# A shared tile for two constants and a gap of 192 bytes: a decoder trunk whose tiles move to other starts in each SBUF partition

## The chip, the core and the metric

The kernel runs on one core of a Trainium2 chip. The metric is the time of one execution on the device in microseconds (us). A NeuronCore has a matrix engine (TensorE: PE for the matmuls, PEld for the loads of their stationary operand), a vector engine (VectorE: DVE), a scalar engine (ScalarE: ACT), GpSimd (POOL), and SyncE (SP), which here issues the DMA transfers. They work side by side and wait for one another on semaphores. Operands lie in SBUF, a memory of 128 partitions; a tile takes the same stretch of bytes in each partition. Matmuls write to PSUM.

## The reference

Two layers of a decoder trunk on 256 tokens of width 2048, float32 throughout. Each sub-layer is `x <- x + gate * f(RMSNorm(x) * (1 + scale) + shift)`, and shift, scale and gate come from a conditioning vector through a large matrix.

```python
cond = jax.nn.silu(c)
for l in range(DEPTH):                                  # 2 layers
    mod = cond @ ada_w[l] + ada_b[l]                    # 2048 -> 6 * 2048
    sh1, sc1, g1, sh2, sc2, g2 = jnp.split(mod, 6, axis=-1)
    h = modulate(rmsnorm(x, norm_mix_g[l]), sh1, sc1)
    y = mixer_ab(h, ...) if l % 2 == 0 else mixer_c(h, ...)
    x = x + g1[:, None, :] * y
    h = modulate(rmsnorm(x, norm_ffn_g[l]), sh2, sc2)
    x = x + g2[:, None, :] * swiglu(h, ffn_w1[l], ffn_w3[l], ffn_w2[l])
return rmsnorm(x, final_g)

def swiglu(h, w1, w3, w2):                              # 2048 -> 5632 -> 2048
    return (jax.nn.silu(h @ w1) * (h @ w3)) @ w2
```

`mixer_ab` is a product with a 2048 x 4096 matrix, a causal convolution over 31 tokens on one half, a gated mixing of tokens on the other, and a product with a 2048 x 2048 matrix. `mixer_c` is a pooling over 2, 4, 8 and 16 tokens and four products with 512 x 512 matrices. Nearly all the work is products of 256 tokens with weight matrices that are read once from the chip's main memory (HBM).

## The kernel before

**Products in three terms.** `load` brings 256 rows x 512 columns of a weight matrix (512 KB) into a tile `raw` of 4096 bytes in each partition; twelve such buffers are in use. `split` cuts it into two float32r tiles: ACT rounds `raw` to `hi` (L206), DVE takes `lo = raw - hi` (L207); four buffers each. The activations are cut in the same way: `ah` and `al` for the inputs of a sub-layer, `mh` and `ml` in the same places for the inner activations of the mixers, `hh` and `hl` for the hidden activations of SwiGLU. For each block of 128 x 128 activations, TensorE loads the block as the stationary operand (LDWEIGHTS, 512 bytes in each partition) and streams 512 columns of weights past it (MATMUL, the moving operand, 2048 bytes in each partition). The three products are high by high (L255), high weights by low activations (L256), and low weights by high activations (L261). So one half of `unit` (one `raw`) is 12 matmuls: for each of two token blocks twice L255 and L256, then four of L261. Rows of the profile name `out<-moving,stationary`: `mm<-hi,hh` streams `hi` past `hh`. `mm` and, in places, `mt` are the PSUM results.

**Stages.** An opening in a written order (conditioning vector, first norms); `mixer_ab` (up to some 440 us); SwiGLU of layer 0 (to about 1190 us); `mixer_c`; SwiGLU of layer 1. In SwiGLU the products with `w1` and `w3` have `ah` and `al` as stationary operands, those with `w2` have `hh` and `hl`. Beside the main products run steps of the conditioning products: on PE (L354, L420) or on DVE (L392, L427), handed out by a credit that `tick` counts.

**Where tiles lie.** Pools are laid out one after the other in each partition in the order in which `__init__` opens them: constants, `x` (residual), `act` (`ah`, `al`, and `mh`, `ml` in the same places), `raw`, `whi` (`hi`), `wlo` (`lo`), `acc`, `gate`, `work`; then a pool of the stage, which for SwiGLU holds `hh` and `hl`, 2048 bytes each. A tile takes its bytes rounded up to 32, so a constant of 4 bytes takes 32. In the program as built, the starts modulo 512 bytes are:

| tiles | before | after |
|---|---|---|
| `ident`, `identr`, `ones` (128 columns each) | 160 | 160 |
| `x`, `ah`/`al`/`mh`/`ml`, `raw`, `hi`, `lo`, `acc`, `gate` | 32 | 0 |
| work tiles `xr`, `gy`, `hm`, `s1` (2048 bytes) | 32 | 192 |
| work tiles `rows`; `h32` | 352; 96 | 0; 256 |
| `hh`, `hl` (SwiGLU), and the bands for `mixer_c` in the same places | 352 | 0 |
| in `mixer_ab`: `aT`, the convolution's input; `co`, its output | 352; 288 | 0; 448 |

The blocks of an activation tile lie 512 bytes apart and the two halves of a weight tile 2048, so all of one family's operands share the start of their family. `mhalf` (-0.5) is read by POOL for the power in `rstd` (L518); `pick` (ones in rows 0, 32, 64, 96) is the moving operand of one column in `put_cols` (L448).

Of the kernel before, what the change touches and what calls it, by code (L numbers as in the profile page):

```python
# [8 lines left out]
F32 = mybir.dt.float32  # L9
# [8 lines left out]
P = 128  # L18
# [22 lines left out]
class Trunk:  # L41
# [6 lines left out]
    def __init__(self, ctx, tc, ins, out):  # L48
        self.ctx, self.tc, self.nc = ctx, tc, tc.nc
        self.i, self.out = ins, out  # L50
        self.bg = []
        self.credit = 0.0
        self.late = []
        self.fill = []
        self.lean = False

        def pool(name, bufs, **kw):
            return ctx.enter_context(tc.tile_pool(name=name, bufs=bufs, **kw))

        self.cpool = pool("const", 1)  # L60
        self.xpool = pool("resid", 1)
        self.apool = pool("act", 1)
        self.rawp = pool("raw", RAW)
        self.hip = pool("whi", HL)
        self.lop = pool("wlo", HL)
        self.accp = pool("acc", 1)
        self.gp = pool("gate", 2)
        self.wk = pool("work", 2)
        self.mmp = pool("mmp", 4, space=PSUM)
        self.tpp = pool("tpp", 2, space=PSUM)  # L70
        self.adap = pool("adap", 1, space=PSUM)
        self.msp = pool("msp", 1, space=PSUM)


    def consts(self):
        nc, c = self.nc, self.cpool
        i = self.i
        warm = c.tile([P, 1], F32, name="warm")
        nc.vector.memset(warm, 0.0)
        nc.scalar.activation(warm, warm, AF.Silu)  # L80
        self.ident = c.tile([P, P], F32, name="ident")
        make_identity(nc, self.ident)
        self.identr = c.tile([P, P], F32R, name="identr")
        nc.vector.tensor_copy(self.identr, self.ident)
        self.ones = c.tile([P, P], F32, name="ones")
        nc.vector.memset(self.ones, 1.0)
        self.mhalf = c.tile([P, 1], F32, name="mhalf")
        nc.gpsimd.memset(self.mhalf, -0.5)
        self.pick = c.tile([P, 1], F32, name="pick")
        nc.gpsimd.memset(self.pick, 0.0)  # L90
        for j in range(4):
            nc.gpsimd.memset(self.pick[32 * j : 32 * j + 1, :], 1.0)
# [1105 lines left out]
```

## Time and profile before

| what | value |
|---|---|
| runs | 2008.52, 2008.23, 2002.36 us; median 2008.23 us |
| the profiled execution | 2001.65 us, span of its instructions 1999.9 us |
| mean granted TensorE clock | 0.984 |
| matmuls | 8896, of which 7584 are of the three kinds L255, L256, L261 |
| moved by DMA | 540.39 MB, 537.79 MB of it on SP's queue |

The page of the profile gives, in this order: the busy time of each engine; the span in 40 equal slices, each digit the busy share in tenths; the DMA queues; the chain of work that ended last, followed back from the end, as shares of the span; the costliest groups of instructions by line and operands with their mean duration. A matmul's duration in these rows is from its start to the modelled end of its results; the next one starts before that, so the pace of a stream is read from the distance between starts in the timeline, not from the duration.

### The profile page before, as it was taken

The numbers are of one execution on the slowest core, as the hardware profiler recorded it, in microseconds if no ns is written. First come the engines' busy times: TensorE is split into PE (matmuls) and PEld (weight loads), VectorE is DVE, ScalarE is ACT, GpSimd is POOL, SyncE is SP. The second block draws the span as 40 slices with busy tenths as digits, with TensorE's granted clock in tenths as the row PEclk, the third lists the DMA queues.
The fourth block names the chain that finished last, engine by engine and source line by source line (L and its number), as shares of the span: only waits on it lengthen the run. The fifth ranks groups of instructions, "written<-read, shape, count | busy, mean of one in ns | idle before, by whom it ended". The sixth has DMA issues, their size and how long they took to land.

```text
span 1999.9 us, 24247 instructions
## 1 busy us (share of the span) xinstructions
PE 1950.2 (98%) x8896; PEld 1539.9 (77%) x8896; DVE 1408.9 (70%) x1650; ACT 849.8 (42%) x1047; POOL 33.9 (2%) x92
## 2 busy tenths in 40 slices
PE   6899999989999999999999999999999999999998
PEld 3566667768887888887878877888788888888886
DVE  2678999796878878777887788877455445554455
ACT  3244343465444334433344346544434444334443
POOL 0000000000000000000210000000000000000000
PEclk7899999989999999999999999999999999999999
DMA  9998988798989899888988887988556665566551
GB/s 350 366 358 281 339 273 277 277 343 278 322 299 327 314 311 347 313 295 304 327 325 297 281 289 264 332 280 309 194 189 190 190 190 191 178 196 192 189 184 48
DMA packets 246248, 540.39 MB, mean 270 GB/s; under 512 B 16521, under 2 KB 17849, under 8 KB 245744
## 3 DMA queue, kind: packets, MB, share of 16 engines
q1 hardware_dynamic: 245840, 537.79, 77.9%
q8 instruction: 69, 1.13, 0.2%
q10 hardware_dynamic: 288, 1.05, 0.1%
q14 instruction: 51, 0.42, 0.1%
HBM read 536.68 MB, written 2.10 MB: 269 GB/s over the span
## 4 chain that ended last, share of the span: by engine, by line
PE 93%; DMA 3%; DVE 2%; ACT 1%; issue 0%; SPq 0%; POOL 0%; POOLq 0%; DVEq 0%; ACTq 0%
PE mm L255 28%; PE mm L256 27%; PE mm L261 27%; PE ps_ada L420 1%; DMA raw<-in_ab_w_in_dram 1%; PE ps_col L448 1%; PE mt L255 1%; PE tp L699 1%; PE mt L256 1%; PE mt L261 1%; PE ps_ada L354 1%; PE tp L532 1%; DMA x<-in_x_dram 1%; DVE accq L427 1%; DMA raw<-in_ada_w_dram 1%; PE tp L965 1%
## 5 line engine op out<-in xcount | busy, mean ns | idle before, releaser
L206 ACT CAST hi<-raw 128x1024 fp32r<-128x1024 f32 x632 | 663.8, 1052 | 1010.9 <-PE mm L256 902.8
L207 DVE TENSOR_TENSOR lo<-raw,hi 128x1024 fp32r<-128x1024 f32 x632 | 771.0, 1224 | 426.0 <-ACT hi L206 419.2
L255 PE MATMUL mm<-hi,ah 128*128 128x512 f32 x1568 | 618.7, 395 | 4.7 <-ACT hi L206 3.7
L256 PE MATMUL mm<-hi,al 128*128 128x512 f32 x1568 | 613.5, 391 | 0.0
L261 PE MATMUL mm<-lo,ah 128*128 128x512 f32 x1568 | 422.1, 390 | 0.0
L255 PEld LDWEIGHTS mm<-hi,ah 128*128 128x128 f32 x1568 | 295.6, 189 | 89.3 <-ACT hi L206 16.0
L261 PEld LDWEIGHTS mm<-lo,ah 128*128 128x128 f32 x1568 | 295.0, 188 | 61.6
L256 PEld LDWEIGHTS mm<-hi,al 128*128 128x128 f32 x1568 | 296.0, 189 | 60.2
L255 PE MATMUL mm<-hi,hh 128*128 128x512 f32 x704 | 278.9, 396 | 0.0
L256 PE MATMUL mm<-hi,hl 128*128 128x512 f32 x704 | 278.1, 395 | 0.0
L392 DVE SCALAR_TENSOR_TENSOR acc<-raw,cond,acc 128x1024 f32<-128x1024 f32 x210 | 269.1, 1281 | 7.0 <-DMA raw<-in_ada_w_dram 5.1
L261 PE MATMUL mm<-lo,hh 128*128 128x512 f32 x704 | 194.7, 395 | 0.0
L255 PEld LDWEIGHTS mm<-hi,hh 128*128 128x128 f32 x704 | 132.0, 187 | 33.9 <-ACT hi L206 1.7
L261 PEld LDWEIGHTS mm<-lo,hh 128*128 128x128 f32 x704 | 132.0, 187 | 32.2
L256 PEld LDWEIGHTS mm<-hi,hl 128*128 128x128 f32 x704 | 132.1, 188 | 31.8
L803 DVE SCALAR_TENSOR_TENSOR co<-aT,cw,co 128x256 f32<-128x256 f32 x240 | 100.1, 484 | 0.0
L420 PE MATMUL ps_ada<-raw,cond 128*32 128x512 f32 x352 | 60.9, 659 | 6.4 <-DMA raw<-in_ada_w_dram 5.7
L255 PE MATMUL mm<-hi,mh 128*128 128x512 f32 x160 | 65.1, 408 | 1.6 <-ACT mh L541 1.6
L256 PE MATMUL mm<-hi,ml 128*128 128x512 f32 x160 | 64.6, 406 | 0.3 <-DVE ml L542 0.3
L707 DVE TENSOR_TENSOR gy<-mm,gate 128x512 f32<-128x512 f32 x72 | 47.0, 686 | 23.9 <-PE mm L261 23.6
L427 DVE SCALAR_TENSOR_TENSOR accq<-raw,cond,accq 128x512 f32<-128x512 f32 x75 | 56.3, 751 | 9.7 <-DMA raw<-in_ada_w_dram 7.8
L255 PE MATMUL mt<-hi,ah 128*128 128x512 f32 x96 | 40.7, 424 | 7.2 <-ACT hi L206 7.2
(170 smaller groups left out, 993.7 us busy)
## 6 DMA issues: line engine op xcount, KB each, us to landing
raw<-in_ffn_w_dram SPq DMA_DIRECT2D x528, 512.0 KB, 4.8
raw<-in_ada_w_dram SPq DMA_DIRECT2D x384, 512.0 KB, 5.6
raw<-in_ab_w_in_dram SPq DMA_DIRECT2D x64, 512.0 KB, 7.9
raw<-in_ab_w_out_dram SPq DMA_DIRECT2D x32, 512.0 KB, 6.6
raw<-in_pool_w_dram SPq DMA_DIRECT2D x8, 512.0 KB
x<-in_x_dram SPq DMA_DIRECT2D x2, 1024.0 KB
gate<-in_final_g_dram SPq DMA_DIRECT2D x1, 1024.0 KB
out_dram<-x SPq DMA_DIRECT2D x2, 512.0 KB, 3.8
```

What stands on the lines that cost most here:

```text
L206: nc.scalar.copy(hi, raw)
L207: nc.vector.tensor_tensor(lo, raw, hi.bitcast(F32), op=ALU.subtract)
L255: nc.tensor.matmul(ps[b], act[b][0][:, kk, :], hi[:, k, :], start=first and kk == 0, stop=False)
L256: nc.tensor.matmul(ps[b], act[b][1][:, kk, :], hi[:, k, :], start=False, stop=False)
L261: self.nc.tensor.matmul(ps[b], act[b][0][:, kk, :], lo[:, k, :], start=False, stop=last and kk == 3)
L354: nc.tensor.matmul(ps[32 * j : 32 * j + 32, :], self.cond[:, k : k + 1].to_broadcast([P, 32]), raws[j // 2][:, j % 2, :], start=k == 0, st ...
L392: nc.vector.scalar_tensor_tensor(acc, raw, self.cond[:, k : k + 1], acc, op0=ALU.mult, op1=ALU.add)
L420: nc.tensor.matmul(acc[32 * j : 32 * j + 32, :], self.cond[:, k : k + 1].to_broadcast([P, 32]), raws[j // 2][:, j % 2, :], start=u == 0, s ...
L427: nc.vector.scalar_tensor_tensor(acc, raws[j // 2][:, j % 2, :], self.cond[:, k : k + 1], acc, op0=ALU.mult, op1=ALU.add)
L448: nc.tensor.matmul(ps[:, a : a + 1], src[:, P * a : P * a + P], one, start=u == 0, stop=u == len(parts) - 1,)
L707: nc.vector.tensor_tensor(t, ps, g[:, 512 * q : 512 * q + 512], op=ALU.mult)
L803: nc.vector.scalar_tensor_tensor(co[:, k, :], src, cw[:, k, j : j + 1], co[:, k, :], op0=ALU.mult, op1=ALU.add,)
```

## The change

Two constants of 4 bytes, `mhalf` and `pick`, become the two columns of one tile `two`, so that the constants take 32 bytes less and all that follows moves down by 32 bytes. At the head of the pool `work` a tile `gap` of 192 bytes is reserved, which nothing reads or writes; with it the pool behind `work` begins 160 bytes further up than before. No instruction is added or taken away, and on every engine the instructions stand in the same order with the same waits; only the name `two` stands where `mhalf` and `pick` stood. The starts that result are in the table above.

```diff
@@ -66,6 +66,7 @@
         self.accp = pool("acc", 1)
         self.gp = pool("gate", 2)
         self.wk = pool("work", 2)
+        self.wk.tile([P, 48], F32, name="gap", tag="gap", bufs=1)
         self.mmp = pool("mmp", 4, space=PSUM)
...
@@ -84,9 +85,9 @@
         nc.vector.memset(self.ones, 1.0)
-        self.mhalf = c.tile([P, 1], F32, name="mhalf")
+        two = c.tile([P, 2], F32, name="two")
+        self.mhalf, self.pick = two[:, :1], two[:, 1:]
         nc.gpsimd.memset(self.mhalf, -0.5)
-        self.pick = c.tile([P, 1], F32, name="pick")
         nc.gpsimd.memset(self.pick, 0.0)
```

## The prediction

> **What bounds the kernel now.** I read the page from the top: busy shares, the slices, the chain.
>
> ```profile
> span 1999.9 us, 24247 instructions
> PE 1950.2 (98%) x8896; PEld 1539.9 (77%) x8896; DVE 1408.9 (70%) x1650; ACT 849.8 (42%) x1047; POOL 33.9 (2%) x92
> PE   6899999989999999999999999999999999999998
> DMA  9998988798989899888988887988556665566551
> PE 93%; DMA 3%; DVE 2%; ACT 1%; issue 0%; SPq 0%; POOL 0%; POOLq 0%; DVEq 0%; ACTq 0%
> ```
>
> PE is busy in 98% of the span, and only the first slices have holes. The chain that ended last lies on PE for 93% and on DMA for 3% (0.03 x 1999.9 = 60 us). The other engines matter only through what they hold up. So I need the pace of the matmul stream, and who works in it:
>
> ```profile
> L255 PE MATMUL mm<-hi,ah 128*128 128x512 f32 x1568 | 618.7, 395 | 4.7 <-ACT hi L206 3.7 <-ACT ah L541 1.0
> L255 PE MATMUL mm<-hi,hh 128*128 128x512 f32 x704 | 278.9, 396 | 0.0
> L255 PE MATMUL mm<-hi,mh 128*128 128x512 f32 x160 | 65.1, 408 | 1.6 <-ACT mh L541 1.6
> L255 PE MATMUL mt<-hi,ah 128*128 128x512 f32 x96 | 40.7, 424 | 7.2 <-ACT hi L206 7.2
> ```
>
> Each of these rows stands for three equal groups (L255, L256, L261). With `ah`/`al` or `mh`/`ml` as stationary operand there are 3 x (1568 + 160 + 96) = 5472 matmuls, with `hh`/`hl` 3 x 704 = 2112. The durations overlap, so they don't tell the pace. The timeline does: the group of four L261 returns every 12 matmuls. First and last rows of undisturbed stretches, `hh` twice, then `ah`, then `mh`:
>
> ```profile
> 640.30 1.09 PE L261 MATMUL mm<-lo,hh 128*128 128x512 f32 x4
> ...
> 679.50 1.09 PE L261 MATMUL mm<-lo,hh 128*128 128x512 f32 x4
> ```
>
> ```profile
> 1457.26 1.09 PE L261 MATMUL mm<-lo,hh 128*128 128x512 f32 x4
> ...
> 1513.26 1.09 PE L261 MATMUL mm<-lo,hh 128*128 128x512 f32 x4
> ```
>
> ```profile
> 551.88 1.07 PE L261 MATMUL mm<-lo,ah 128*128 128x512 f32 x4
> ...
> 568.20 1.07 PE L261 MATMUL mm<-lo,ah 128*128 128x512 f32 x4
> ```
>
> ```profile
> 398.10 1.07 PE L261 MATMUL mm<-lo,mh 128*128 128x512 f32 x4
> ...
> 411.70 1.07 PE L261 MATMUL mm<-lo,mh 128*128 128x512 f32 x4
> ```
>
> The stretches hold 14, 20, 6 and 5 returns. With `hh`: 39.20 / 14 = 2.80 us and 56.00 / 20 = 2.80 us for 12 matmuls, 233.3 ns each. With `ah`: 16.32 / 6 = 2.72 us; with `mh`: 13.60 / 5 = 2.72 us, 226.7 ns each. The same moving tiles `hi` and `lo` run 6.67 ns slower past one family of stationary operands than past the others. Is that other work beside it?
>
> ```profile
> 551.00:569.00 18.00, 18.00 (x81) 14.81 (x79) 8.02 (x7) 7.88 (x9) 0.00 (x0) 1.00 0.67 214
> 640.00:680.00 40.00, 40.00 (x173) 32.22 (x173) 32.83 (x32) 15.03 (x15) 0.00 (x0) 1.00 0.93 341
> 1457.00:1514.00 57.00, 57.00 (x246) 45.69 (x245) 30.81 (x31) 21.49 (x21) 0.00 (x0) 1.00 0.58 186
> ```
>
> (Stretch and its length; then busy time and, in brackets, instructions of PE, PEld, DVE, ACT, POOL; then granted clock, DMA share, GB/s.) No: the clock is 1.00 in all three, and `hh` goes at 2.80 us both beside 341 GB/s and a DVE at 82% and beside 186 GB/s and a DVE at 54%, while `ah` at 2.72 lies between them in DMA. Nor is the load of the stationary operand itself longer (minimum, median and maximum in ns, from the rows of L255):
>
> ```profile
> L255 PEld LDWEIGHTS mm<-hi,ah x1568: 186/188/330, 44.3 to 1920.7; 128*128 128x128 f32 x196
> L255 PEld LDWEIGHTS mm<-hi,hh x704: 186/187/192, 621.2 to 1989.2; 128*128 128x128 f32 x176
> ```
>
> What the layout sets apart is the start: `hi`, `lo`, `ah` and `mh` all begin at 32 modulo 512 bytes, `hh` at 352. A load of stationary values runs under the stream of the matmul before it, so both read SBUF at once; an offset of 320 between them seems to cost 6.67 ns a matmul, an offset of 0 does not.
>
> The Trainium skill, in "TensorE: Matmul & The Clock Gate", section "Back-to-back issue gap", gives a gap of N/2.4 + 2.5 ns for an isolated matmul on the full clock, 216 ns for 512 columns, with no term for where the operands lie. By it the change would be worth nothing on TensorE. The trace does not agree with it: 226.7 and 233.3 ns.
>
> **The change, part by part.**
>
> *The starts of `hh` and `hl`* go from 352 to 0, those of `hi` and `lo` from 32 to 0: the offset between them becomes 0, as it is now between `hi` and `ah`. Bounds: 0 (the pace has another cause) and the full difference, 2112 x 6.67 ns = 14.1 us. I take 14.1, since two families at offset 0 (`ah`, `mh`, with different data) keep 226.7 to the last digit. All of it lies on the path: PE is busy without a hole in both `hh` stretches. What is late next there: ACT's `hi` waits for PE, so it follows; DMA would have to give 341 x 2.80 / 2.72 = 351 GB/s in the first stretch, below what it gives in the opening (387 below).
>
> *The starts of `hi`, `lo`, `ah`, `al`, `mh`, `ml`* go together from 32 to 0. Their offset to each other stays 0. No row shows a family that starts at 0; the rows around are 226.7 (at 32) and 233.3 (at 352). Below, the quickest stream of loads and matmuls is the plain float32 one of the convolution's norm:
>
> ```profile
> 347.10 2.32 PE L813 MATMUL ps_ln<-co,ones 128*128 128x256 f32 x10
> L813 PE MATMUL ps_ln<-co,ones 128*128 128x256 f32 x16 | 3.9, 379 | 0.0
> ```
>
> Ten take 2.32 us, the last of them 0.38: (2.32 - 0.38) / 9 = 215.5 ns each, for half as many columns of another type, but one full load beneath each as here. So the ends for these 5472 are 5472 x (215.5 - 226.7) = -61 us and 5472 x (233.3 - 226.7) = +36.5 us. I take 0, the nearest row, their own: if the offset between two streams decides, nothing changes.
>
> *DVE and ACT.* All their operands move. L803 reads the convolution's input at starts that step by 4 bytes from tap to tap, and L207, between tiles that all start at 32, is as even:
>
> ```profile
> L803 DVE SCALAR_TENSOR_TENSOR co<-aT,cw,co x240: 432/483/510, 167.0 to 347.9; 128x256 f32<-128x256 f32 x120
> L207 DVE TENSOR_TENSOR lo<-raw,hi x632: 1211/1225/1362, 44.2 to 1979.5; 128x1024 fp32r<-128x1024 f32 x158
> ```
>
> Thirty starts, and all lie between 432 and 510 ns, so DVE hardly sees the start; for ACT no row varies it. The chain has DVE and ACT for 3% (60 us); 1% of that either way is 0.6 us. I take 0.
>
> *DMA.* Every `raw` is now written from a multiple of 512. What this brings shows only where a transfer is waited for, and that is the opening:
>
> ```profile
> ACT hi L206 <- DMA raw<-in_ab_w_in_dram: 42.3, 10, 11.2
> 0.00:20.00 20.00, 9.50 (x33) 2.15 (x33) 2.63 (x10) 7.62 (x20) 3.44 (x17) 0.90 0.90 337
> 20.00:40.00 20.00, 17.02 (x85) 8.72 (x87) 3.55 (x13) 5.59 (x11) 0.55 (x1) 0.67 0.97 344
> 40.00:60.00 20.00, 17.92 (x72) 11.40 (x72) 15.67 (x22) 6.68 (x10) 0.00 (x0) 0.75 1.05 387
> 60.00:80.00 20.00, 15.82 (x69) 10.60 (x62) 11.37 (x19) 7.37 (x11) 1.10 (x1) 0.83 0.98 334
> ```
>
> The rate is 337 to 387 GB/s at one and the same start. If all four stretches (mean 350.5) went at the best, the 60 us of DMA on the chain would shrink by 60 x (1 - 350.5/387) = 5.7 us; that is the end for a gain. If all went at the worst, it would grow by 60 x (350.5/334 - 1) = 3 us, the end for a loss. I take a gain of 1 us, near the middle.
>
> The Trainium skill ("DMA: Bandwidth & Descriptors", section "How a descriptor splits into AXI transactions") says that a piece that starts off a 256-byte boundary is cut at the boundary below: 2048 bytes from 32 would take 65 beats of 32 bytes instead of 64. By that, an estimate, the gain would be 60 / 65 = 0.9 us. No run here shows a transfer into SBUF from such a boundary.
>
> *The shared tile and the gap* add no instruction or wait. POOL's power and PE's one-column products read the same values; both constants are written once in the opening, in the same order on POOL. 0.
>
> *Transposes* read work tiles that start at 192 instead of 32, against `ident` at 160. The two large groups:
>
> ```profile
> L699 PE MATMUL tp<-ident,hm 128*128 128x128 f32 x176 | 23.1, 272 | 0.0
> L532 PE MATMUL tp<-ident,xr 128*128 128x128 f32 x96 | 18.5, 342 | 9.9 <-ACT xr L527 6.6 <-ACT xT L570 3.1
> ```
>
> At 6.67 ns each, either way, 272 of them are 2 us. I take 0.
>
> **The sum** is made against the profiled execution: 2001.65 - 14.1 - 1 = 1986.6 us. Runs shown reach from 2002.36 to 2008.52 with the median 6.6 us above the profiled time. Half of that on top gives 1990.
>
> **The rivals.**
>
> *The start itself decides, and 0 is good for all.* Then `ah` and `mh` gain too. For it: 226.7 is 11.2 ns above the 215.5 of L813, and everything in that stream starts off a 64-byte multiple (32, 352). Against it: 32 and 352 are equally odd for any line of 64 bytes, and yet differ. Halfway between the ends, 221 ns for all: 5472 x 5.6 + 2112 x 12.3 = 57 us, so 1945 us; at the end 61 + 2112 x 17.8 ns = 99 us, and DVE, at 82% in one stretch above, would take part of that back.
>
> *Nothing happens.* The `hh` tiles also lie in the last part of the partition, behind `work`, and stay there; if that, or their values, set the pace, only DMA's 1 us is left: 2001, or up to 2008 on the scale of the median.
>
> *Slower: 0 is the bad start.* If two streams that begin on the same 512-byte multiple hinder each other as 352 and 32 do now, `ah` and `mh` go to 233.3: 5472 x 6.67 = 36.5 us, and `hh` stays: 2038 us. It decides from the point where the 456 groups of 12 with `ah` or `mh` lose more than the `hh` groups and DMA bring: 15.1 us / 456 = 33 ns a group, 2.753 instead of 2.72. For it: no row shows a start at 0. Against it: `hi` and `ah` now also begin on the same place of their 512 bytes, and are the quicker ones.
>
> **How the numbers follow.** Offset decides, 1990: 0.60, between 1983 (DMA's full gain, on the profiled time) and 1997 (on the median, without DMA's). All gain, 1945: 0.16. Nothing: 0.15. Slower: 0.09. A measurement of this kernel can tell about 0.3%, 6 us. The range 1940 to 2008 leaves out the slower case and the far half of the all-gain case, 0.17 together. Faster by over 0.3%: 0.16, all but a little of 0.60, and 0.02 of "nothing" by scatter, 0.73; within: 0.18; slower: 0.09.
>
> **What would show it.** In the profile of the changed kernel: groups of L261 with `hh` every 2.72 us, those with `ah` and `mh` still at 2.72; the same 8896 matmuls; durations of L206 and L207 as now; the waits for `raw` in the opening within a few us of 42. The prediction is wrong if `hh` stays at 2.80 (the place in the partition or the data), or if `ah` leaves 2.72 in either direction (the start itself).

## The result, and the profile after

The changed kernel took 1985.13 us (median of four runs, 1983.53 to 1990.03) against 2006.13 for the kernel before (with a fourth run of 2004.03): a ratio of 0.9901, 95% interval 0.9875 to 0.9927. A second comparison of the same two kernels gave 0.9895 (0.9881 to 0.9910). The forecast was 1990 us, and 15.1 of 2001.65 us, 0.75%, by its sum; the ratio says 1.0%.

The page of the changed kernel, its span, PE's busy share, the chain and the group with `hh`:

```profile
span 1988.3 us, 24247 instructions
PE 1940.1 (98%) x8896; PEld 1541.6 (78%) x8896; DVE 1407.9 (71%) x1650; ACT 852.1 (43%) x1047; POOL 34.5 (2%) x92
PE 93%; DMA 3%; DVE 1%; ACT 1%; issue 0%; SPq 0%; POOL 0%; POOLq 0%; ACTq 0%; DVEq 0%
L256 PE MATMUL mm<-hi,hh 128*128 128x512 f32 x704 | 275.2, 391 | 0.0
```

The same instructions, the same bound. (One line was added to the code, so L255, L256, L261 and L206 of before are L256, L257, L262 and L207 here.) What changed is the pace past `hh`. The group of four `lo` matmuls returns every 12 matmuls. The first and the last such group of undisturbed stretches, with `hh`, then `ah`, then `mh`:

```profile
1452.22 1.07 PE L262 MATMUL mm<-lo,hh 128*128 128x512 f32 x4
...
1506.62 1.07 PE L262 MATMUL mm<-lo,hh 128*128 128x512 f32 x4
```

```profile
548.17 1.07 PE L262 MATMUL mm<-lo,ah 128*128 128x512 f32 x4
...
569.93 1.07 PE L262 MATMUL mm<-lo,ah 128*128 128x512 f32 x4
```

```profile
393.57 1.07 PE L262 MATMUL mm<-lo,mh 128*128 128x512 f32 x4
...
409.89 1.07 PE L262 MATMUL mm<-lo,mh 128*128 128x512 f32 x4
```

With `hh` 20 returns take 54.40 us, 2.72 each, where they took 2.80 before. `ah` (21.76 / 8) and `mh` (16.32 / 6) stay at 2.72. It is not the clock: the granted clock was 1.00 in the stretch with `hh`, as it was before (behind the five busy times, clock, DMA share and GB/s):

```profile
1452.00:1507.00 55.00, 55.00 (x244) 45.57 (x243) 30.82 (x31) 21.29 (x21) 0.00 (x0) 1.00 0.61 192
```

What that is worth in all can be read from the first write of an `hh` tile, which stands ahead of every matmul with `hh`, to the end of the span. First and last start of the 44 writes, before and then after:

```profile
L700 ACT CAST hh<-tp x44: 585/592/606, 513.6 to 1929.0; 128x512 fp32r<-128x512 f32 x44
L701 ACT CAST hh<-tp x44: 586/592/605, 515.2 to 1919.3; 128x512 fp32r<-128x512 f32 x44
```

1999.9 - 513.6 = 1486.3 us became 1988.3 - 515.2 = 1473.1: 13.2 us less, with a granted clock of 1.00 from there on in both. If each of the 2112 matmuls with `hh` or `hl` gave up the 6.67 ns it would be 14.1.

Ahead of that lies the opening. Stretches of 20 us there, last column GB/s:

```profile
0.00:20.00 20.00, 10.64 (x33) 2.81 (x33) 2.84 (x11) 7.88 (x21) 3.44 (x17) 0.91 0.90 348
20.00:40.00 20.00, 17.26 (x91) 7.99 (x91) 4.34 (x14) 7.33 (x15) 0.55 (x1) 0.70 0.95 360
40.00:60.00 20.00, 17.42 (x74) 11.52 (x72) 16.83 (x24) 4.68 (x6) 0.00 (x0) 0.79 1.05 406
60.00:80.00 20.00, 14.23 (x58) 9.36 (x59) 11.25 (x18) 7.57 (x11) 1.63 (x1) 0.83 0.94 330
```

337, 344, 387 and 334 became 348, 360, 406 and 330. Where the DMA engines are busy throughout (share over 1), 387 became 406, 5% more. The chain of waits through the opening, start and length of pieces that wait for weights, before and then after:

```profile
78.30 10.74 DMA raw<-in_ada_w_dram
89.10 10.76 DMA raw<-in_ab_w_in_dram
```

```profile
76.11 10.22 DMA raw<-in_ada_w_dram
86.39 10.22 DMA raw<-in_ab_w_in_dram
```

Each is 5% shorter, and the second ends at 96.6 us instead of 99.9. This lead of 3 us did not last. The same eight `hi` matmuls and the `lo` group behind them, before and then after, with the granted clock around them (the number ahead of the DMA share):

```profile
119.16 0.39 PE L255 MATMUL mm<-hi,ah 128*128 128x512 f32 x1
121.01 1.07 PE L261 MATMUL mm<-lo,ah 128*128 128x512 f32 x4
115.00:120.00 5.00, 3.23 (x13) 2.14 (x13) 4.86 (x8) 0.64 (x2) 0.00 (x0) 1.00 1.01 368
```

```profile
116.78 0.63 PE L256 MATMUL mm<-hi,ah 128*128 128x512 f32 x1
120.18 1.09 PE L262 MATMUL mm<-lo,ah 128*128 128x512 f32 x4
115.00:120.00 5.00, 4.04 (x10) 3.03 (x11) 4.89 (x8) 2.48 (x3) 0.00 (x0) 0.67 1.05 406
```

They begin 2.4 us earlier, but at a granted clock of 0.67 instead of 1.00 they take 3.40 us instead of 1.85, and 0.8 us of the lead is left. A later stretch took that too:

```profile
320.00:425.00 105.00, 103.14 (x487) 77.94 (x485) 90.50 (x121) 44.15 (x61) 1.61 (x1) 0.97 0.84 296
```

```profile
320.00:425.00 105.00, 103.14 (x475) 77.34 (x473) 90.40 (x121) 43.60 (x61) 1.61 (x1) 0.95 0.83 290
```

(Before, then after: 487 matmuls at a granted clock of 0.97, 475 at 0.95.) At the first `hh` this execution was 1.6 us behind the one before (515.2 and 513.6). The two profiled executions are therefore only 2001.65 - 1990.03 = 11.6 us apart, while the medians are 21.0. The one shown here is the longest of its four runs.

### The profile page after: what moved, and what is told of

Read it like the earlier page. It is cut to its first block, busy times and chain, and to the rows that moved or that the text cites. A ratio compares the mean times of both kernels' runs of the same rounds, so it can differ in the third digit from the quotient of the medians.

```text
span 1988.3 us, 24247 instructions
## 1 busy us (share of the span) xinstructions
PE 1940.1 (98%) x8896; PEld 1541.6 (78%) x8896; DVE 1407.9 (71%) x1650; ACT 852.1 (43%) x1047; POOL 34.5 (2%) x92
## 4 chain that ended last, share of the span: by engine, by line
PE 93%; DMA 3%; DVE 1%; ACT 1%; issue 0%; SPq 0%; POOL 0%; POOLq 0%; ACTq 0%; DVEq 0%
PE mm L256 28%; PE mm L257 27%; PE mm L262 27%; PE ps_ada L421 2%; PE ps_col L449 1%; DMA raw<-in_ada_w_dram 1%; PE tp L700 1%; PE mt L256 1%; PE mt L257 1%; PE mt L262 1%; PE ps_ada L355 1%; DMA raw<-in_ab_w_in_dram 1%; PE tp L533 1%; DMA x<-in_x_dram 1%; PE tp L966 1%
## 5 line engine op out<-in xcount | busy, mean ns | idle before, releaser
L207 ACT CAST hi<-raw 128x1024 fp32r<-128x1024 f32 x632 | 665.8, 1054 | 997.0 <-PE mm L257 892.8
L256 PE MATMUL mm<-hi,ah 128*128 128x512 f32 x1568 | 619.4, 395 | 4.7 <-ACT hi L207 3.7
L257 PE MATMUL mm<-hi,al 128*128 128x512 f32 x1568 | 614.1, 392 | 0.0
L262 PE MATMUL mm<-lo,ah 128*128 128x512 f32 x1568 | 422.2, 390 | 0.0
L256 PEld LDWEIGHTS mm<-hi,ah 128*128 128x128 f32 x1568 | 296.1, 189 | 90.3 <-ACT hi L207 15.1
L257 PEld LDWEIGHTS mm<-hi,al 128*128 128x128 f32 x1568 | 296.4, 189 | 60.3
L262 PEld LDWEIGHTS mm<-lo,ah 128*128 128x128 f32 x1568 | 294.9, 188 | 61.7
L256 PE MATMUL mm<-hi,hh 128*128 128x512 f32 x704 | 275.2, 391 | 0.0
L257 PE MATMUL mm<-hi,hl 128*128 128x512 f32 x704 | 274.2, 389 | 0.0
L262 PE MATMUL mm<-lo,hh 128*128 128x512 f32 x704 | 190.3, 389 | 0.0
L256 PEld LDWEIGHTS mm<-hi,hh 128*128 128x128 f32 x704 | 132.2, 188 | 29.6 <-ACT hi L207 1.7
L262 PEld LDWEIGHTS mm<-lo,hh 128*128 128x128 f32 x704 | 132.1, 188 | 27.6
L257 PEld LDWEIGHTS mm<-hi,hl 128*128 128x128 f32 x704 | 132.2, 188 | 27.1
L256 PE MATMUL mm<-hi,mh 128*128 128x512 f32 x160 | 65.1, 408 | 1.6 <-ACT mh L542 1.6
L257 PE MATMUL mm<-hi,ml 128*128 128x512 f32 x160 | 64.1, 403 | 0.3 <-DVE ml L543 0.3
L262 PE MATMUL mm<-lo,mh 128*128 128x512 f32 x160 | 47.3, 405 | 0.0
```

The source lines that it names most:

```text
L207: nc.scalar.copy(hi, raw)
L256: nc.tensor.matmul(ps[b], act[b][0][:, kk, :], hi[:, k, :], start=first and kk == 0, stop=False)
L257: nc.tensor.matmul(ps[b], act[b][1][:, kk, :], hi[:, k, :], start=False, stop=False)
L262: self.nc.tensor.matmul(ps[b], act[b][0][:, kk, :], lo[:, k, :], start=False, stop=last and kk == 3)
```

## The experiments

**The two edits apart.** Theory: the offset between the moving and the stationary operand decides. Rival: the multiple of 512 itself. The gap alone brings offset 0 without a multiple of 512 (`hi` and `hh` both at 32); the shared tile alone brings `hi` to 0 and leaves the offset at 320.

```diff
 # gap_only: before, with
+        self.wk.tile([P, 48], F32, name="gap", tag="gap", bufs=1)
 # two_only: before, with
+        two = c.tile([P, 2], F32, name="two")
+        self.mhalf, self.pick = two[:, :1], two[:, 1:]
```

> The gap of 192 bytes alone, the two constants in tiles of their own as before. `hi`, `lo`, `ah`, `raw` stay at 32 modulo 512, `hh` and `hl` go from 352 to 32. If the offset between the stationary operand and the moving one decides, groups of 12 matmuls with `hh` return every 2.72 us, and the kernel gains the 14.1 us of TensorE alone: ratio to the kernel before about 0.993. If the multiple of 512 itself decides, `hh` keeps 2.80 and the ratio is 1.000.

> The shared tile alone, no gap. `hi`, `lo`, `ah`, `raw` go to 0, `hh` and `hl` to 320: the offset between them stays 320. If the offset decides, `hh` keeps 2.80 us for 12 matmuls, `ah` 2.72, and what is left is the effect of writing `raw` to a multiple of 512: 1 us by the prediction (ratio 0.9995), up to 5.7 us (0.997) if the whole rest of the measured gain is that. If the start itself decides, `hh` changes its pace.

The gap alone: ratio 0.9936 (0.9922 to 0.9950). The shared tile alone: 0.9969 (0.9958 to 0.9979). `hh` in the timeline of each, 22 groups, first the gap alone, then the shared tile alone:

```profile
1450.83 1.07 PE L262 MATMUL mm<-lo,hh 128*128 128x512 f32 x4
...
1507.95 1.07 PE L262 MATMUL mm<-lo,hh 128*128 128x512 f32 x4
```

```profile
1450.18 1.09 PE L261 MATMUL mm<-lo,hh 128*128 128x512 f32 x4
...
1508.98 1.09 PE L261 MATMUL mm<-lo,hh 128*128 128x512 f32 x4
```

57.12 / 21 = 2.72 with the gap, 58.80 / 21 = 2.80 with the shared tile. The offset decides, and a start at 32 is as good as one at 0. From the first `hh` to the end the gap alone takes 1473.3 us, like the changed kernel, and the shared tile alone 1486.2, like the kernel before. So what the shared tile brings, by the ratio 2004 x 0.0031 = 6.2 us, lies ahead of the first `hh`: it comes at 509.2 us instead of 513.6 in the profiled executions. The two parts add up: 0.64% and 0.31% against the 1.0% of both.

**Which offsets are good.** Pads between the chunks of `hh` and `hl` give four offsets to `hi` in one kernel.

```diff
 # ffn, ahead of the tiles of chunk ci in the first group of layer 0
+                if gi == 0 and l == 0 and (BASE if ci == 0 else 64):
+                    p.tile([P, (BASE if ci == 0 else 64) // 4], F32, name=f"pad{ci}", tag=f"pad{ci}")
```

> The changed kernel with pads between the SwiGLU tiles, so that the four chunks of hidden activations start at 0, 64, 128 and 192 modulo 512, while `hi` and `lo` stay at 0. If two streams hinder each other in narrow places of the 512 bytes, only some of the four chunks run at more than 2.72 us for 12 matmuls. If any offset costs, three of the four do. If the part of the partition decides, all four run alike.

> As the kernel with starts 0 to 192, but the chunks start at 256, 320, 384 and 448 modulo 512. The offset theory expects 2.80 us for 12 matmuls at 320, as in the kernel before; for the others it has no number. If a start that is odd to 64 bytes was the cause (352 before), all four run at 2.72.

> The four chunks of hidden activations at 32, 96, 160 and 224 modulo 512, with `hi` and `lo` at 0. The scan in steps of 64 gave 226.7, 233.3, 232.3 and 229.9 ns a matmul at 0, 64, 128 and 192. If the cost rises and falls evenly, 32 lies between 226.7 and 233.3 and 224 between 229.9 and 226.7; if offset 0 is a single good place, all four lie at 230 to 233. One below 226.7 would be a better place than the changed kernel's.

Each chunk is two halves of 12 matmuls, so two returns of `lo` belong to one chunk; the distance inside a pair is that chunk's pace. Offsets 0, 64, 128, 192, a pair each:

```profile
1452.37 1.07 PE L262 MATMUL mm<-lo,hh 128*128 128x512 f32 x4
1455.09 1.07 PE L262 MATMUL mm<-lo,hh 128*128 128x512 f32 x4
1457.86 1.10 PE L262 MATMUL mm<-lo,hh 128*128 128x512 f32 x4
1460.66 1.09 PE L262 MATMUL mm<-lo,hh 128*128 128x512 f32 x4
1463.44 1.10 PE L262 MATMUL mm<-lo,hh 128*128 128x512 f32 x4
1466.24 1.08 PE L262 MATMUL mm<-lo,hh 128*128 128x512 f32 x4
1469.00 1.08 PE L262 MATMUL mm<-lo,hh 128*128 128x512 f32 x4
1471.75 1.08 PE L262 MATMUL mm<-lo,hh 128*128 128x512 f32 x4
```

2.72, 2.80, 2.80 and 2.75 us. In the second kernel the pair at 256:

```profile
1453.74 1.07 PE L262 MATMUL mm<-lo,hh 128*128 128x512 f32 x4
1456.46 1.07 PE L262 MATMUL mm<-lo,hh 128*128 128x512 f32 x4
```

2.72 again; its other three pairs repeat the first kernel's (2.81, 2.80, 2.75). So the pattern has a period of 256 bytes, and 320 before was 64. At 32, 96, 160 and 224, 17 groups from the third kernel:

```profile
1448.18 1.09 PE L262 MATMUL mm<-lo,hh 128*128 128x512 f32 x4
...
1493.00 1.10 PE L262 MATMUL mm<-lo,hh 128*128 128x512 f32 x4
```

44.82 / 16 = 2.80. Of the eight offsets modulo 256 that were tried, 0 alone runs at 2.72, and none is below. (A chunk lasts 24 matmuls and follows one at another offset; what a longer stretch at one offset, 192 above all, would hold was not run.) The kernels took 1994.01, 1995.37 and 1998.13 us, one run each.

**The same cost put on the other operands.** If the offset decides, it must also slow `ah` and `mh` when these are the ones left behind. (`self.hip`, `self.lop` and `self.accp` are the pools of `hi`, `lo` and `acc`; what is reserved at the head of a pool moves all that lies behind it.)

```diff
 # hi_gap192: after, with
         self.hip = pool("whi", HL)
+        self.hip.tile([P, 48], F32, name="gap_hip", tag="gap_hip", bufs=1)
 # lo_gap192: after, with 48 such elements at the head of self.lop and 16 at the head of self.accp
```

> The changed kernel with 192 bytes more ahead of `hi`: `raw` and `ah` stay at 0, while `hi`, `lo`, `hh` and all that follows start at 192 modulo 512. From `hi` to `ah` the offset is then -192, which is 64 modulo 256, the place at which the scan ran slow; from `hi` to `hh` it is 0. If the offset modulo 256 decides, `ah` and `mh` now take 2.80 us for 12 matmuls and `hh` 2.72: 36.5 us more than the changed kernel, about 2022 us, a ratio of 1.008 to 1.010 to the kernel before. If only the far tiles behind the work pool are sensitive, `ah` keeps 2.72 and the time is that of the changed kernel.

> The changed kernel with `lo` alone moved, to 192 modulo 512; `hi`, `raw` and `ah` at 0, `hh` at 256, which is 0 modulo 256 from `hi`. From `lo` to all stationary operands the offset is then 64 modulo 256. If the moving tile's offset to the stationary block that is loaded beneath it decides, the four matmuls that stream `lo` run at 233.3 ns and the eight that stream `hi` at 226.7: 2.75 us for 12, 16.9 us more in all, about 2002 us. If the bare position of `hh` or `ah` decides, nothing changes.

With `hi` and `lo` moved, `ah` (9 groups) and `hh` (20 groups):

```profile
548.87 1.09 PE L263 MATMUL mm<-lo,ah 128*128 128x512 f32 x4
...
571.27 1.09 PE L263 MATMUL mm<-lo,ah 128*128 128x512 f32 x4
...
1454.76 1.08 PE L263 MATMUL mm<-lo,hh 128*128 128x512 f32 x4
...
1506.44 1.07 PE L263 MATMUL mm<-lo,hh 128*128 128x512 f32 x4
```

22.40 / 8 = 2.80 and 51.68 / 19 = 2.72: the roles are exchanged. The time is 2018.85 us (ratio 1.0071, 1.0050 to 1.0092), 34 us above the changed kernel's 1984.58; 5472 x 6.67 ns would be 36.5. With `lo` alone moved:

```profile
1649.81 0.40 PE L259 MATMUL mm<-hi,al 128*128 128x512 f32 x1
...
1651.42 1.09 PE L264 MATMUL mm<-lo,ah 128*128 128x512 f32 x4
1652.35 0.39 PE L258 MATMUL mm<-hi,ah 128*128 128x512 f32 x1
```

The four that stream `lo` take 0.93 us, 232.5 ns each, as expected. But the seven of `hi` ahead of them take 1.61, 230.0 ns each and not 226.7: after a stretch of bad offset it takes some matmuls until the good pace is back. So the 12 take more than the 2.75 us expected:

```profile
1453.25 1.09 PE L264 MATMUL mm<-lo,hh 128*128 128x512 f32 x4
...
1505.82 1.09 PE L264 MATMUL mm<-lo,hh 128*128 128x512 f32 x4
```

52.57 / 19 = 2.767 us. Over all 632 groups of 12 that would be 29.5 us; the one run took 2008.10 us, 18 to 25 us above the runs of the changed kernel, where 16.9 were expected. So the tile that streams matters and not only the one that is loaded; how the delay carries over stays open.

**What a transfer needs.** `raw` (pool `self.rawp`) at 64 and at 256 modulo 512, the operands of the main products at offset 0 modulo 256 to each other.

```diff
 # raw64: after, with 16 elements at the head of self.rawp and 48 at the head of self.hip
 # raw256: after, with 64 elements at the head of self.rawp
```

> The changed kernel with `raw` at 64 modulo 512, and `hi`, `lo`, `hh` at 256, so that their offset to `ah` stays 0 modulo 256. TensorE keeps 2.72 us for 12 matmuls with all. If it takes a multiple of 256 for a transfer to be quick, as the Trainium skill has it (page DMA: Bandwidth & Descriptors), the opening is as slow as with the start at 32 and the ratio to the kernel before is 0.993 to 0.994, as with the gap alone; if a multiple of 64 is enough, it is 0.990 to 0.991.

> As the kernel with `raw` at 64, but at 256 modulo 512. If a multiple of 256 is enough for DMA and an offset of 256 is 0 for TensorE, the ratio is that of the changed kernel, 0.990; if it takes 512, 0.993 to 0.994.

Ratios 0.9925 (0.9911 to 0.9938) and 0.9912 (0.9896 to 0.9928), whose intervals overlap. The opening tells them apart, GB/s in the last column; first 64, then 256:

```profile
40.00:60.00 20.00, 17.61 (x80) 10.66 (x74) 15.42 (x21) 6.43 (x10) 0.00 (x0) 0.81 1.05 387
80.00:100.00 20.00, 15.58 (x78) 10.08 (x76) 12.65 (x18) 2.09 (x2) 0.00 (x0) 0.91 1.05 387
```

```profile
40.00:60.00 20.00, 15.62 (x74) 9.48 (x72) 16.26 (x21) 4.61 (x5) 0.00 (x0) 0.97 1.05 406
80.00:100.00 20.00, 14.51 (x71) 8.96 (x70) 14.85 (x19) 4.67 (x5) 0.00 (x0) 0.89 1.05 408
```

387 is the rate of the start at 32, 406 to 408 that of the start at 0. The other runs agree: in these two stretches all three kernels with `raw` at 32 or 64 show 387, and all nine with it at 0 or 256 show 401 to 408. A multiple of 64 is not enough, one of 256 is; 128 was not tried. The Trainium skill ("DMA: Bandwidth & Descriptors", section "How a descriptor splits into AXI transactions") puts the boundary at 256 bytes too, but speaks of bytes that are fetched, and here it is the destination that moved. An estimate by its count of beats, 65 from 32 and 66 from 64 against 64, is 1.6% and 3%; the runs show 5% at both.

In the time it is harder to see. In the profiled executions the first `hh` is written at 513.6 (before), 513.9 (gap alone) and 517.8 us (`raw` at 64), and at 515.2 and 512.8 (changed kernel, twice), 514.7 (`raw` at 256) and 509.2 (shared tile alone): the two sets overlap, and the executions differ in the clock that was granted (0.982 to 0.986 on the mean).

**Is there more to have?** All the remaining large tiles at 0 as well, beside the changed kernel on the same chip.

```diff
 # all0: after, without the gap in work; gs.., sh.., cond, adab, two, warm reserved ahead of ident;
 # 48 elements at the head of the pools "ffn" and "ab", 16 behind aT
```

> The changed kernel with the rest put in place too: the small constants are reserved ahead of `ident`, `identr` and `ones`, which with `xr`, `gy`, `hm`, `s1` and the convolution's `wcT`, `prm`, `co` then also start at 0 modulo 512 (`hh`, `hi`, `ah`, `raw` stay there); the gap moves behind the work pool. If only the offset between `hi`/`lo` and their stationary operands and the start of `raw` matter, the time is that of the changed kernel within 0.2%. If transposes, DVE or ACT gain from starts at 0 as well, up to 0.3% more, 0.987 of the kernel before.

> The changed kernel once more, on the chip of the kernel with all tiles at 0, for a direct comparison: 0.990 of the kernel before.

0.9899 (0.9883 to 0.9915) with all at 0, and 0.9895 (0.9881 to 0.9910) for the changed kernel. From the first `hh` to the end they take 1473.1 and 1473.0 us. The starts of the other tiles bring nothing that can be measured, and no kernel tried beats the changed one.

## Why the prediction was right

*`hh` and `hl`, 14.1 us.* Right in mechanism and nearly so in size: 2.80 went to 2.72, the stretch from the first `hh` to the end lost 13.2 us, and the gap alone measured 0.64%, 12.8 us (interval 10.0 to 15.6). The reading that carried it was the distance of starts. The group's mean duration, 396 ns with `hh` and 395 with `ah` before, would have hidden it.

*`ah`, `mh` unchanged, 0.* Right. The forecast named the offset modulo 512; the period is 256. For this change that made no difference, since both 320 and 64 lie at the bad pace.

*DMA, 1 us.* This term was too small. The price was found from the spread of rates at one start, as if the start brought a small share of it; its end for a gain, 5.7 us, took 387 GB/s for the best rate. In its place the runs show a rate that rises by 5%, to 406, wherever the DMA engines are full. Two waits of 10.75 us became 10.22, and at 96.6 us the profile was some 3 us ahead; lower granted clocks behind that place took it back in this execution. By the ratios the term is 6.2 us (4.2 to 8.4, shared tile alone), 8 us (changed kernel against gap alone, 0.9895 and 0.9936) or 2.6 us (`raw` at 256 against 64). These figures scatter too much to say more than a few us, and where what exceeds the 3 us lies was not found.

*DVE, ACT, transposes, constants read from the shared tile, 0.* Right within the measurement, though not taken apart: all tiles at 0 gave nothing more.

*The rivals.* That the start itself decides fell with the gap alone (start 32, pace 2.72). That `hh`'s place in the partition or its values set the pace fell with the scan: the same tiles in the same region go at 2.72, 2.75 or 2.80. That 0 is a bad start fell with the profile after. That the change is worth nothing on TensorE, as by the gap of an isolated matmul in the Trainium skill ("TensorE: Matmul & The Clock Gate", section "Back-to-back issue gap"), fell too: addresses alone moved the pace of this stream both ways.

*The scale.* Half of the 6.6 us between the profiled time and the median was put on top; the median came out 1.5 us below even the sum on the profiled time. That DMA brought more would do it, but the runs of one kernel lie 6 us apart, so that 1990 came within 5 us of 1985 is in part luck.

## What to carry to other kernels

When TensorE runs without holes, read its pace from the distance of starts, by family of operands; where families that do the same work differ, try their addresses. For float32r matmuls of 512 columns, lay moving and stationary tiles so that their starts agree modulo 256 bytes, and let tiles that large transfers write start at multiples of 256. Both cost nothing here but a few bytes of padding, and small constants at the head of a partition can undo them unseen.

## What the runs showed of the hardware that was not expected

- The pace of the stream depends on the offset from the moving to the stationary tile, with a period of 256 bytes: 2.72 us for 12 matmuls at 0, 2.75 at 192, 2.80 at 64, 128 and the odd multiples of 32. What inside SBUF or TensorE causes it was not tried.
- The delay outlives its cause: after four matmuls at a bad offset and one more, the next seven at a good one averaged 230.0 ns instead of 226.7.
- A lead won in the opening can be lost to the clock: the same eight matmuls began 2.4 us earlier, met a granted clock of 0.67 instead of 1.00, and kept 0.8 us of it.
- The transfers of weights in the opening, in pieces of 2048 bytes, go at 387 GB/s to starts at 32 or 64 and at 401 to 408 to multiples of 256, where the DMA engines are full.
